# A two-layer hybrid decoder step: first loads by quarters, the table stage moved and shortened, the last gate by token parts

## Chip, cores, metric

One core of a Trainium2 chip. The metric is the device time of one execution in microseconds (us). Smaller is better. The median of the kernel before is 1286.86 us over 3 runs (1286.62 to 1287.45).

## What is computed

One inference step of a decoder with two layers, for 256 prompt tokens and 8 times 8 sample tokens (320 in all), width 1024. The reference, cut to the parts that the change touches:

```python
def layer(x, p, lw, h0, cache_k, cache_v):
    x = x + 0.5 * swiglu(rms_norm(x, lw['ffn1_norm']), lw['ffn1_w_gate'], lw['ffn1_w_up'], lw['ffn1_w_down'])
    mix, new_k, new_v, h_last = token_mixer(rms_norm(x, lw['mix_norm']), lw, h0, cache_k, cache_v)
    x = x + mix
    x = x + 0.5 * swiglu(rms_norm(x, lw['ffn2_norm']), lw['ffn2_w_gate'], lw['ffn2_w_up'], lw['ffn2_w_down'])
    gate = jax.nn.sigmoid((rms_norm(x, lw['ple_norm']) @ lw['ple_w_gate']).astype(F32))
    x = x + ((p @ lw['ple_w_proj']).astype(F32) * gate).astype(x.dtype)
    return x, new_k, new_v, h_last
...
    a_bar = jnp.exp(lam * dt)
    b_bar = ((a_bar - 1.0) / lam)[..., None] * b
...
    _, h = lax.associative_scan(_ssm_combine, (a, bu), axis=0)
...
    y_prompt = rms_norm(xp, final_norm)
```

`token_mixer` projects to u, q, k and v, runs an S5 state space model (32 groups of 16 channels with 64 complex states) on u and sliding-window attention on q, k, v, takes the RMS norm of each result and projects both back. A feed-forward part has 2816 hidden columns, 22 blocks of 128.

## The kernel before

Activations lie transposed, 128 rows of the width on the partitions and the 320 tokens along the free axis, so x is eight blocks `x[0]` to `x[7]` in one tile `xa`. Weights are streamed: SP loads a block of 128 x 1024 fp32 into one of four tiles `wr` (`wfetch`, L159), ScalarE rounds it to the high half `wh` (L163), VectorE subtracts to get the low half `wl` (L164), and two blocks are held ahead (`wtake`). The normed input of a product is split in the same way (`Norm.cut`: high half on ScalarE at L225, low half on VectorE at L226). `mm3` then makes each 128 x 128 x 320 product as three matmuls: high by high (L182), high by low (L183), low by high (L184).

A norm is never applied to the input itself. `Norm.stat` squares each block (ScalarE, L210) and adds it to `acc` (VectorE, L216); `Norm.finish` sums over partitions with matmuls by a column of ones (L244), forms the mean square on VectorE (L247) and the power -0.5 on POOL (L249). The spread of that factor over the partitions by transposes (L267) is held back by `LATER` = 22 further matmuls (24, since they come in threes), and multiplies the products when they leave PSUM.

A layer is a first feed-forward part, the mixer, a second feed-forward part and the gate (`ple`). In `ffn` the gate and up products of 12 blocks are followed by 8 down products, then 10 blocks and again 8. After each block's activation and each down product `step` asks the generator `prep` for its next piece: `prep` builds the tables of the state space model for a layer on VectorE, POOL, ScalarE and with a few transposes on TensorE, the first layer's in its own first feed-forward part (38 steps), the second layer's in the first layer's second feed-forward part. Its last pieces are the tables of cosines and sines `ect` and `est` (32 groups by 32 positions): five doublings (L579 to L584) and two renormalisations of 16 columns each (L590 to L595). `tt_d`, a table in memory, is filled with zeros (2 x 2 MB from a zeroed `wr`) before its non-zero parts are written by eight gathers.

Instructions are written in the order of this description and a scheduler places them on the engines; in the mixer a written sequence (`MIXSEQ`) sets the order of the pieces. At the start x comes in three loads and the first two weight blocks in two halves each (`HEAD`), all on SP, and the squares of the first norm are made partly on POOL (L212, L216). At the end, the eight products of the last gate are followed by the sigmoid chain of block 7 (L999 to L1002), the square, the final norm and the products with the final factor (L1058), stored in four pieces (L1059).

## Time and profile before

| | |
|---|---|
| median of 3 runs | 1286.86 us |
| profiled execution | 1286.57 us |
| its span, first to last instruction | 1284.8 us |
| granted TensorE clock, mean | 0.995 of 2.4 GHz |
| TensorE matmul / weight load busy | 98% / 96% |
| VectorE / ScalarE / POOL busy | 71% / 47% / 6% |
| memory traffic | 210.62 MB, 164 GB/s |

The profile is that of one execution. PE is TensorE, PEld its weight loads, DVE VectorE, ACT ScalarE, SP the engine that issues most loads. A row of the timeline gives the start, the duration and, in brackets, how long the engine sat idle before and what released it. Matmuls are pipelined: one of 320 columns has a duration of 0.31 us while the next starts after less than half of that, so the distance of two starts tells the pace and not the duration.

### The profile page before, as it was taken

To read this page: it belongs to the slowest core of one execution; us is meant where nothing else is said; L and a number is where in the kernel's file an instruction comes from. 1 tells how busy PE (TensorE), PEld (TensorE's weight loads), DVE (VectorE), ACT (ScalarE), POOL (GpSimd) and SP (SyncE) were. 2 spreads that over 40 slices of the span, in tenths; PEclk is the share of its full clock that TensorE was granted. 3 is DMA by queue.
4 is the path that set the end of the run, shared out by engine and by line. 5 is a ranking of instruction groups with operands and counts; after the bars stand their busy time and mean duration, and the time that the engine had idled before them with its cause. 6 is when DMAs were issued, how large, how long until landed. Compare 5 with 4: busy or idle time off the path is not lost.

```text
span 1284.8 us, 22994 instructions
## 1 busy us (share of the span) xinstructions
PE 1257.4 (98%) x9153; PEld 1231.1 (96%) x9153; DVE 911.0 (71%) x1609; ACT 598.9 (47%) x984; POOL 81.5 (6%) x96
## 2 busy tenths in 40 slices
PE   7999999899999999999999999999999999999996
PEld 7999999898899999999999999999888999999996
DVE  6588776978786878788785555557877755555575
ACT  5443433455764443344653333345476543333454
POOL 4300002001004000010000000000000000000000
PEclk9999999999999999999999999999999999999998
DMA  7836666354254468654444454345432444454351
GB/s 251 314 125 204 240 208 212 120 197 144 76 192 147 150 194 256 219 189 141 166 174 151 129 154 174 136 115 188 164 106 99 147 151 135 142 180 141 113 174 41
DMA packets 74620, 210.62 MB, mean 164 GB/s; under 512 B 8545, under 2 KB 18497, under 8 KB 74481
## 3 DMA queue, kind: packets, MB, share of 16 engines
q1 hardware_dynamic: 72560, 203.22, 47.8%
q0 software_dynamic: 1664, 5.28, 1.3%
q8 instruction: 72, 1.18, 0.4%
q10 hardware_dynamic: 288, 0.66, 0.1%
q14 instruction: 36, 0.29, 0.1%
HBM read 191.78 MB, written 19.69 MB: 165 GB/s over the span
## 4 chain that ended last, share of the span: by engine, by line
PE 89%; DVE 6%; issue 3%; ACT 1%; POOL 1%; DMA 0%; SPq 0%; POOLq 0%; DVEq 0%; ACTq 0%
PE pt L182 17%; PE pt L184 17%; PE pt L183 17%; PE pc L182 11%; PE pc L184 11%; PE pc L183 11%; DVE wl L164 2%; PE pa L872 1%; PE pa L500 1%; POOL r L249 1%; DVE s L704 0%; DVE s L703 0%; DMA xa<-xT 0%; PE pa L883 0%; PE pa L244 0%
## 5 line engine op out<-in xcount | busy, mean ns | idle before, releaser
L163 ACT ACTIVATE wh<-wr 128x1024 fp32r<-128x1024 f32 (+3 forms) x365 | 350.9, 963 | 556.3 <-issue 302.0
L184 PE MATMUL pt<-big,wl 128*128 128x320 f32 x1584 | 492.6, 311 | 4.3 <-DVE wl L164 4.3
L182 PE MATMUL pt<-big,wh 128*128 128x320 f32 x1584 | 493.4, 312 | 0.0
L183 PE MATMUL pt<-big,wh 128*128 128x320 f32 x1584 | 492.2, 311 | 0.0
L164 DVE TENSOR_TENSOR wl<-wr,wh 128x1024 fp32r<-128x1024 f32 (+3 forms) x365 | 403.1, 1107 | 100.5 <-ACT wh L163 98.5
L182 PE MATMUL pc<-big,wh 128*128 128x320 f32 x992 | 310.7, 314 | 6.7 <-ACT wh L163 6.0
L183 PE MATMUL pc<-big,wh 128*128 128x320 f32 x992 | 308.8, 312 | 0.0
L184 PE MATMUL pc<-big,wl 128*128 128x320 f32 x992 | 308.2, 311 | 0.0
L184 PEld LDWEIGHTS pt<-big,wl 128*128 128x128 f32 x1584 | 298.8, 189 | 6.0 <-DVE wl L164 5.5
L183 PEld LDWEIGHTS pt<-big,wh 128*128 128x128 f32 x1584 | 299.1, 189 | 0.5
L182 PEld LDWEIGHTS pt<-big,wh 128*128 128x128 f32 x1584 | 298.8, 189 | 0.7 <-issue 0.4
L182 PEld LDWEIGHTS pc<-big,wh 128*128 128x128 f32 x992 | 187.2, 189 | 9.6 <-ACT wh L163 6.2
L183 PEld LDWEIGHTS pc<-big,wh 128*128 128x128 f32 x992 | 187.1, 189 | 1.2 <-DVE big L226 1.2
L184 PEld LDWEIGHTS pc<-big,wl 128*128 128x128 f32 x992 | 187.2, 189 | 0.6 <-issue 0.3
L291 DVE TENSOR_TENSOR fa<-pt,ft 128x320 f32<-128x320 f32 x88 | 43.0, 489 | 91.0 <-PE pt L184 90.5
L288 DVE TENSOR_TENSOR ft<-pc,r 128x320 f32<-128x320 f32 x88 | 42.6, 488 | 53.6 <-PE pc L184 53.5
L334 DVE SCALAR_TENSOR_TENSOR fd<-pt,r 128x320 f32<-128x320 f32 x64 | 31.3, 490 | 31.6 <-PE pt L184 31.6
L249 POOL TENSOR_TENSOR r<-ms,mhalf 107x3 f32<-107x3 f32 x13 | 17.1, 1319 | 565.0 <-DVE ms L247 565.0
L225 ACT ACTIVATE big<-xa,prm 128x320 fp32r<-128x320 f32 x64 | 35.3, 559 | 31.4 <-DVE xa L335 17.4
L295 ACT ACTIVATE big<-fa 128x320 fp32r<-128x320 f32 x88 | 40.2, 459 | 14.6 <-DVE fa L291 14.5
L289 ACT ACTIVATE ft<-ft 128x320 f32<-128x320 f32 x88 | 40.0, 458 | 13.1 <-DVE ft L288 13.0
L226 DVE SCALAR_TENSOR_TENSOR big<-xa,prm,big 128x320 fp32r<-128x320 f32 x64 | 37.9, 599 | 8.4 <-ACT big L225 8.4
(246 smaller groups left out, 904.6 us busy)
## 6 DMA issues: line engine op xcount, KB each, us to landing
wr<-f1u SPq DMA_DIRECT2D x44, 512.0 KB, 3.2
wr<-f2g SPq DMA_DIRECT2D x44, 512.0 KB, 3.3
wr<-f2u SPq DMA_DIRECT2D x44, 512.0 KB, 3.3
wr<-f1g SPq DMA_DIRECT2D x43, 512.0 KB, 3.3
wr<-f1d SPq DMA_DIRECT2D x32, 384.0 KB, 3.1
wr<-f2d SPq DMA_DIRECT2D x32, 384.0 KB, 3.1
wr<-f1d SPq DMA_DIRECT2D x32, 320.0 KB, 2.9
wr<-win SPq DMA_DIRECT2D x20, 512.0 KB, 3.8
```

Of the source, the lines that this page charges most:

```text
L163: S.activation(h[:, c], raw[:, c], AF.Copy)
L164: i = V.tensor_tensor(lo[:, c], raw[:, c], h[:, c].bitcast(F32), op=OP.subtract)
L182: PE.matmul(ps, h[:, c], xh, start=start and k == 0, stop=False)
L183: PE.matmul(ps, h[:, c], xl, start=False, stop=False)
L184: PE.matmul(ps, lo[:, c], xh, start=False, stop=stop and k == n - 1)
L225: S.activation(h, src, AF.Copy, scale=g)
L226: V.scalar_tensor_tensor(lo, src, g, h.bitcast(F32), op0=OP.mult, op1=OP.subtract)
L288: V.tensor_tensor(t, pg, r, op=OP.mult)
L289: S.activation(t, t, AF.Silu)
L291: V.tensor_tensor(a, pu, t, op=OP.mult)
L295: S.activation(h, a, AF.Copy)
L334: V.scalar_tensor_tensor(t, pd, 0.5, r, op0=OP.mult, op1=OP.mult)
```

## The change

1. **Start.** x and the first two weight blocks are loaded in quarters, prm first; three quarters of x go over the queue of ScalarE. 14 matmuls of zeros (`NWARM`) run on TensorE while the loads are under way. The first pair of products is made quarter by quarter, its two results in turn. The squares of the first norm come after that pair and on ScalarE and VectorE, not on POOL.
2. **Tables.** In `prep` the stage of cosines and sines follows the powers directly. It normalises the one column of 32 elements from which the others are made, not 32 columns at the end. The products for K come before those for Wb. `kt_d` has rows of 240 with a zero part of 112, so each gather reads whole pieces of 128 and `tt_d` needs no zeros. The generator is done after 32 calls for the first layer instead of 36.
3. **Attention squares** are made per block, as soon as a block is there (`attn_stat`), not all at `attn_norm`.
4. `LATER` is 18; two loads (`h0`, `pT`) are issued after the last weight load.
5. **End.** The last gate's blocks 6 and 7 are made in two parts of 192 and 128 tokens (`CUT`). The norm's sums of part 0 run ahead of the last 24 matmuls, the final gain is applied per block, and the output is stored in two pieces of part 0 and three of part 1.

```diff
-LATER = 22
+NWARM = 14
+LATER = 18
+CUT = ((0, 192, 96), (192, 128, 128))
...
+    nc.sync.dma_start(prm, I["prm"])
+    for q in range(4):
+        (S if q < 3 else nc.sync).dma_start(xa[:, 2 * q : 2 * q + 2], I["xT"][:, 2 * q : 2 * q + 2])
+        for raw, src in zip(first, firstw):
+            headdma.append(nc.sync.dma_start(raw[:, 256 * q : 256 * q + 256],
+                                             src[:, 256 * q : 256 * q + 256]).ins)
...
+    pz = pst("po")
+    for _ in range(NWARM):
+        PE.matmul(pz[:, :T], zr_[:, :P], zr_, start=True, stop=True)
...
-                    for k0, k1 in ((0, KCUT), (KCUT, 8)):
+                    ks = (0, 2, 4, 6, 8) if head else (0, KCUT, 8)
+                    for k0, k1 in zip(ks, ks[1:]):
...
-    kt_d = [dram.tile([512, P], F32, name=f"ktd{l}") for l in range(L)]
+    kt_d = [dram.tile([512, 240], F32, name=f"ktd{l}") for l in range(L)]
...
-                nc.sync.dma_start(tt_d[ll].rearrange("p (b c) -> p b c", b=4),
-                                  zt.unsqueeze(1).to_broadcast([P, 4, 1024]))
...
+                nc.sync.dma_start(kt_d[ll].rearrange("(p b) c -> p b c", b=4)[:, :, 0:112], zt)
...
+        V.tensor_tensor(t, uc, uc, op=OP.mult)
+        V.tensor_tensor(er, us, us, op=OP.mult)
+        V.tensor_tensor(t, t, er, op=OP.add)
+        V.tensor_scalar(t, t, -0.5, 1.5, op0=OP.mult, op1=OP.add)
+        V.tensor_tensor(ct_[:, :, 1], uc, t, op=OP.mult)
+        V.tensor_tensor(sn_[:, :, 1], us, t, op=OP.mult)
...
-            PO.dma_start(dst[:, :, i * 16 :], src[:, :, : (8 - i) * 16])
+            PO.dma_start(dst, src[:, :, (7 - i) * 16 : (7 - i) * 16 + P])
...
-        for c0 in (0, 16):
-            cc, ss = ct_[:, :, c0 : c0 + 16], sn_[:, :, c0 : c0 + 16]
-            q1, q2 = auxt("s", [P, G, 16]), auxt("p", [P, G, 16])
-            V.tensor_tensor(q1, cc, cc, op=OP.mult)
-            V.tensor_tensor(q2, ss, ss, op=OP.mult)
-            V.tensor_tensor(q1, q1, q2, op=OP.add)
-            V.tensor_scalar(q1, q1, -0.5, 1.5, op0=OP.mult, op1=OP.add)
-            V.tensor_tensor(cc, cc, q1, op=OP.mult)
-            V.tensor_tensor(ss, ss, q1, op=OP.mult)
...
         def attn_norm():
-            for m in range(4):
-                na.stat(ya[:, m, :])
...
+        if tail is not None:
+            ws = [wtake(), wtake()]
+            pgs = [pst("pc")[:, :T], pst("pt")[:, :T]]
+            for i, ts in enumerate(slice(t0, t0 + n) for t0, n, _ in CUT):
+                xt = [(h[:, ts], lo[:, ts]) for h, lo in xs]
+                for m, w, pg in zip((6, 7), ws, pgs):
+                    mm3(pg[:, ts], *w, 0, xt, True, True)
+                    if i == 1 and m == 6:
+                        tail.sums(0)
+                    gate(m, pg, ts)
+                    tail.stat(i, m, ts)
+            tail.behind = done[-1]
...
+    last.sums(1)
+    last.out(0, ((0, 3), (3, 8)))
+    last.out(1, ((0, 3), (3, 6), (6, 8)))
```

How the instructions move is shown at three places. Line numbers of the changed kernel are its own: L207 to L209 are `mm3`'s three matmuls, L173 the low half of a weight block, L371, L372, L256 and L246 what were L334, L335, L226 and L216.

TensorE at the start of the program, after the change (`zr` is a tile of zeros, `pc` and `pt` the two results of the first pair):

```order
L106 MATMUL po_102<-zr 128x320 x14
L207 MATMUL pc_194<-big_146,wh_142 128x320
L208 MATMUL pc_194<-big_147,wh_142 128x320
L207 MATMUL pt_195<-big_146,wh_144 128x320
L208 MATMUL pt_195<-big_147,wh_144 128x320
L209 MATMUL pc_194<-big_146,wl_143 128x320
```

Before, the program began on TensorE with the products of `pc` alone; now the zeros come first, and products of both results follow as their quarter is there.

VectorE at the end of the first feed-forward part of layer 0, in the second half's down steps, before (`ect`, `est` are the cosines and sines, `wl` the low half of a weight block that TensorE takes next):

```order
L584 TENSOR_TENSOR est_2527<-p_2685,p_2686 128x32x15
L164 TENSOR_TENSOR wl_2697<-wr_2694,wh_2696 128x640
L164 TENSOR_TENSOR wl_2718<-wr_2715,wh_2717 128x640
L334 SCALAR_TENSOR_TENSOR fd_2736<-pt_2693,r_306 128x320
L590 TENSOR_TENSOR s_2744<-ect_2526 128x512
L335 TENSOR_TENSOR xa<-xa,fd_2736 128x320
L591 TENSOR_TENSOR p_2745<-est_2527 128x512
L164 TENSOR_TENSOR wl_2756<-wr_2753,wh_2755 128x640
```

and the same place after the change:

```order
L371 SCALAR_TENSOR_TENSOR fd_2674<-pt_2631,r_335 128x320
L372 TENSOR_TENSOR xa<-xa,fd_2674 128x320
L173 TENSOR_TENSOR wl_2707<-wr_2704,wh_2706 128x640
L256 SCALAR_TENSOR_TENSOR big_2610<-xa,prm,big_2609 128x320
L246 TENSOR_TENSOR acc_2613<-acc_2613,sq_2679 128x320
L173 TENSOR_TENSOR wl_2737<-wr_2734,wh_2736 128x640
```

No product of the tables is left between the low halves.

TensorE at the end of the program, after the change (`po` and `pa` hold the sums and the spread factor; 24 matmuls of 128 columns for block 7 stand between the two groups of L1110):

```order
L209 MATMUL pc_14166<-big_13752,wl_14089 128x128
L1110 MATMUL pa_14257<-ones,acc_14025 96x1
L1110 MATMUL pa_14257<-ones,sq_14230 96x1
...
L209 MATMUL pt_14167<-big_13752,wl_14129 128x128
L1110 MATMUL po_14307<-ones,acc_14025 128x1
L1122 MATMUL pa_14314<-ident,r_2381_14264 128x96 x2
L1110 MATMUL po_14307<-ones,sq_14304 128x1
L1122 MATMUL po_14323<-ident,r_2388_14312 128x128
```

Before, the six sums and the three transposes all stood behind the last matmul; now four sums stand ahead of the last 24.

## Rows read from the trace of the kernel before

**Rows 1.** The page: busy time by engine; the chain's shares
```profile
PE 1257.4 (98%) x9153; PEld 1231.1 (96%) x9153; DVE 911.0 (71%) x1609; ACT 598.9 (47%) x984; POOL 81.5 (6%) x96
...
PE 89%; DVE 6%; issue 3%; ACT 1%; POOL 1%; DMA 0%; SPq 0%; POOLq 0%; DVEq 0%; ACTq 0%
```

**Rows 2.** TensorE's waits: engine, line, awaited line, total us, times, longest
```profile
PE pc L182 <- ACT wh L163: 6.0, 1, 6.0
PE pt L184 <- DVE wl L164: 4.3, 4, 1.9
PE pa L267 <- POOL r L249: 4.3, 5, 1.3
```

**Rows 3.** Timeline of TensorE in the head
```profile
17.22 0.47 PE L182 MATMUL pt<-big,wh 128*128 128x320 f32 x1
17.48 0.47 PE L183 MATMUL pt<-big,wh 128*128 128x320 f32 x1
...
19.57 0.31 PE L182 MATMUL pt<-big,wh 128*128 128x320 f32 x1
...
31.32 0.31 PE L184 MATMUL pc<-big,wl 128*128 128x320 f32 x1
```

**Rows 4.** Busy time by stretch: us, PE, PEld, DVE, ACT, POOL, clock, DMA share, GB/s
```profile
222.00:258.00 36.00, 31.88 (x201) 30.72 (x200) 35.77 (x87) 15.48 (x26) 1.21 (x4) 0.95 0.41 126
66.00:108.00 42.00, 42.00 (x288) 42.00 (x287) 37.78 (x111) 16.23 (x23) 0.00 (x0) 1.00 0.40 123
241.40:244.80 3.40, 3.40 (x14) 3.40 (x14) 3.40 (x7) 1.55 (x3) 0.00 (x0) 0.50 0.61 191
```

**Rows 5.** Timeline of TensorE, table stage
```profile
238.05 0.31 PE L183 MATMUL pt<-big,wh 128*128 128x320 f32 x1
240.24 0.41 PE L184 MATMUL pt<-big,wl 128*128 128x320 f32 x1 [1.88 <-DVE wl L164]
```

**Rows 6.** Timeline of VectorE, same stage
```profile
228.69 0.30 DVE L583 TENSOR_TENSOR ect<-s,s 128x128 f32<-128x128 f32 x1
...
230.61 0.55 DVE L226 SCALAR_TENSOR_TENSOR big<-xa,prm,big 128x320 fp32r<-128x320 f32 x1
...
239.37 1.55 DVE L164 TENSOR_TENSOR wl<-wr,wh 128x640 fp32r<-128x640 f32 x2
...
241.24 0.68 DVE L590 TENSOR_TENSOR s<-ect 128x512 f32<-128x512 f32 x1
```

**Rows 7.** Timeline of ScalarE and VectorE in the head
```profile
4.06 1.01 ACT L225 ACTIVATE big<-xa,prm 128x320 fp32r<-128x320 f32 x2 [1.82 <-DMA prm<-prm]
...
5.99 0.68 DVE L164 TENSOR_TENSOR wl<-wr,wh 128x512 fp32r<-128x512 f32 x1
...
11.51 1.74 DVE L164 TENSOR_TENSOR wl<-wr,wh 128x1024 fp32r<-128x1024 f32 x1
```

**Rows 8.** Timeline of TensorE at a norm in layer 0's mixer
```profile
348.20 0.40 PE L183 MATMUL pc<-big,wh 128*128 128x320 f32 x1
...
349.74 0.49 PE L267 MATMUL pa<-ident,r 107*128 107x107 f32 x3 [0.86 <-POOL r L249]
```

**Rows 9.** Timeline of the end: last two blocks and what follows
```profile
1264.72 0.31 PE L182 MATMUL pc<-big,wh 128*128 128x320 f32 x1
...
1271.61 0.31 PE L184 MATMUL pt<-big,wl 128*128 128x320 f32 x1
...
1274.56 0.35 PE L244 MATMUL pa<-ones,sq 128*107 128x1 f32 x2 [2.54 <-ACT sq L210]
...
1276.01 0.85 POOL L249 TENSOR_TENSOR r<-ms,mhalf 107x3 f32<-107x3 f32 x1 [24.41 <-DVE ms L247]
...
1277.75 3.01 DVE L1058 TENSOR_TENSOR big<-xa,pa 128x320 f32<-128x320 f32 x4 [1.82 <-PE pa L267]
```

**Rows 10.** Timeline of TensorE: narrow operations of layer 0
```profile
109.79 1.04 PE L500 MATMUL pa<-ident,s 128*128 128x128 f32 x8
...
325.97 0.66 PE L811 MATMUL pt<-kv,qs 128*128 128x64 f32 x4
```

More of the change, by code (lines that the diff above doesn't have):

```diff
@@ L1 @@
 import math
-from contextlib import ExitStack
+from contextlib import ExitStack, nullcontext
 import numpy as np
@@ L174, in wtake @@
         return wready.pop(0)
-    waiting = []
+    waiting, held = [], []
     def mm3(ps, h, lo, off, pairs, start, stop):
@@ L187, in mm3 @@
                 if waiting[0][0] <= 0:
-                    waiting.pop(0)[1]()
+                    with tc.issue_after(mm.ins):
+                        waiting.pop(0)[1]()
     class Norm:
@@ L236, in pairs, with finish @@
             ]
-        def finish(self, then=None):
+        def finish(self, then=None, hold=0):
             ps = pst("pa")
@@ L243, in finish @@
                 for i, a in enumerate(sums):
-                    PE.matmul(ps[:SN, c : c + 1], a[:, t0 : t0 + SN], ones, start=i == 0,
+                    mm = PE.matmul(ps[:SN, c : c + 1], a[:, t0 : t0 + SN], ones, start=i == 0,
                               stop=i == len(sums) - 1)
@@ L260, in later @@
                 then(r)
-            waiting.append([LATER, later])
+            waiting.append([hold or LATER, later])
+            if hold:
+                held[:] = [mm.ins, hold]
         def spread(self, r4):
@@ L269, in spread, with ffn @@
             return pr[:, :T]
-    def ffn(l, idx, pre, post, side=None, after=3):
+    def ffn(l, idx, pre, post, side=None, after=3, head=False):
         xs = pre.pairs()
@@ new lines, in hybrid_step_kernel @@
+    pre = Norm(8, lambda m: gcol(0, GF1, m))
+    for raw in first:
+        next(wsrc)
+        wready.append((wpool.tile([P, 1024], F32R, name=nm("wh"), tag="wh", bufs=WB),
+                       wpool.tile([P, 1024], F32R, name=nm("wl"), tag="wl", bufs=WB)))
+    lastdma.extend(headdma)
+    for q in range(4):
+        pre.cut(2 * q, x[2 * q])
+        for raw, (h, lo) in zip(first, wready):
+            wsplit(h, lo, raw, slice(256 * q, 256 * q + 256))
+        pre.cut(2 * q + 1, x[2 * q + 1])
```

317 lines of the change are left out of this document (188 added, 129 removed).

## The prediction

> **What bounds the kernel now.** I read the page's busy shares first and its chain of waits second [rows 1]: TensorE is busy for 98% of the span and the chain that ends last lies on it for 89%, VectorE for 6%. The reader is to see that VectorE, at 71%, is far from full as an average, so a microsecond is worth something only where TensorE does not run at its usual pace. The next view, TensorE's own waits [rows 2], says how few such places there are: one long wait for the first split weights, 4.3 us in four waits for the low half of a weight block (L164), and 4.3 us in five waits for a norm's power (L249), of which the last belongs to the program's end.
>
> Then the timeline of each place. At the usual pace matmuls of 320 columns start 0.147 us apart: 47 intervals between 1264.72 and 1271.61 [rows 9]. **Head:** at 17.22 and 17.48 they start 0.26 apart, at 31.32 the 114th of them starts [rows 3]. At 0.147 each, 114 would take 16.8 us, so the first 31 us hold some 14 us that are not matmuls at pace: waiting for data until 5.99 (the one 6.0 wait [rows 2]), gaps, and the slow pace until 19.35. **Table stage:** between 222 and 258 us VectorE is busy for 35.77 of 36 us and TensorE for 31.88 [rows 4]; a matmul that should start at 238.20 starts at 240.24, behind L164 [rows 5], which itself stands behind the table's products on VectorE [rows 6]. From 241.4 to 244.8 the granted clock is 0.50, its lower level of 1.2 GHz, right after that idle stretch [rows 4]. **Tail:** from the last matmul's start at 1271.61 to the end of the span at 1284.8 are 13.2 us of one short chain after another [rows 9].
>
> **The change part by part.** All sums are against the profiled execution, 1286.57 us (span 1284.8 and 1.8 outside it); the median of the three runs is 0.3 higher.
>
> *Head.* ScalarE and VectorE must make the split inputs and weights of the first pair whatever the size of the loads. Per quarter ScalarE has two L225 (1.01 for two) and two splits of 256 columns, at about 0.4 each: 1.8 us [rows 7]. VectorE has two residuals at 0.55 [rows 6] and two splits at about 0.4 each, from 0.68 for 512 columns [rows 7], which I take for ScalarE too: 1.9. Before, the loads came in another order and POOL's squares ran beside VectorE, where a split of 1024 took 1.74 [rows 7], 1.7 ns a column against 1.2 in the 1.55 for two of 640 [rows 6]. ScalarE starts at 4.06 now, when prm is there; I keep that, since prm is now first and the first part of x is as large as it was. Four quarters at 1.85 and VectorE's lag of 0.6 put the last piece at 12.1 and the 48th product at 13.0. The 14 matmuls of zeros cost 14 times 0.267, 3.7 us, from about 1.5, when VectorE has made the zeros, to 5.25, in time in which TensorE had nothing to do. With them TensorE works almost without a pause from 1.5 on. Before, the fast pace began only at 19.57, when it had run back to back since 15.9; I expect it by about 8. Then 56 products at 0.147 (8.2) reach the 104th, three sums 0.5, nine products 1.3, a wait of 0.5 for the power, since nine products cover less than the 1.5 that this chain takes in the mixer (from 348.20, the first matmul behind the sums, to 349.74 [rows 8]) and VectorE has a split ahead of it, and 0.45 of transposes: the 114th starts at 24.2 instead of 31.32, **-7.1**. Bounds: if the slow pace holds through all 48 products, 12.8 us from 5.3 on, they end at 18.1 and the gain is 2.0; if the splits come faster and it is never slow, 7.9. The squares of the first norm, moved to ScalarE and VectorE, lie behind the splits of the next weights and have 56 products of cover: nothing.
>
> *Tables.* Twelve products of 512 columns go (L590 to L595, 0.68 each [rows 6]), replaced by six of 32 columns, and the rest of that stage moves into the first twelve activation steps. In the last six down steps VectorE then has only its two splits (1.55 together), and four operations near 0.4 to 0.5: 3.2 us in a step whose 30 matmuls take 4.4. So no wait stays there. The four waits cost 4.3, some 0.12 more each from start to start (2.04 for the longest, where the row says 1.88), 4.8; the 14 matmuls at the lower clock took 3.4 us, 2.06 at the usual pace, 1.3. Together **-6.1**. What it costs if the cover is gone: from 66 to 108 us VectorE was already busy for 37.78 of 42 us [rows 4]. Priced with such rows, the table work of the generator's calls 6 to 12 comes to some 23 us; seven steps of 48 matmuls are 49.3 us, of which VectorE's own two splits and three operations leave about half, 24.7. The 4 MB of zeros that went to memory from SP become 0.46 MB; the loads that follow on SP are not late, since two blocks are held ahead. The eight gathers on POOL stay eight. The same generator in layer 0's second FFN caused no wait before and is shorter now: nothing.
>
> *Norms in the mixer.* The attention squares leave VectorE's queue ahead of the sums, so the sums come earlier: 14 matmuls ahead of the third, but then four before the transposes where three stood. The chain from sums to transposes is as long, and its wait (0.86 at 349.74 [rows 8]) is shortened by one matmul in each layer: **-0.3** for both. The order around it is changed too; I bound that by 1 us a layer either way. The delay of 18 instead of 24 matmuls elsewhere still covers the chain: nothing.
>
> *Tail.* 48 matmuls of 320 columns become 48 of 192 and 48 of 128. The trace has no narrow product of this kind. The nearest row is the transposes of 128 by 128 that load 128 columns of weights each [rows 10]: eight in 1.04 us, the last taking 0.27, so 0.110 apart. 96 times 0.110 is 10.6 against 48 times 0.147, 7.05: +3.5. I take that value for both widths, since every matmul still loads 128 columns. Bounds: 0.147, as for the wide ones, +7.1; and in proportion to the columns (0.088 and 0.059), nothing. Four more sums calls in mid-stream, whose two records take 0.35 [rows 9] and overlap their neighbours for more than half of it, 0.15 each: +0.6. After the last matmul, 2.95 us to the sums before [rows 9] were 0.35 to the first operation and five steps of 0.52; five of 0.33 for 128 columns (0.30 for one on VectorE [rows 6]) make 2.0; one sums call, ms and power (0.85) lead to 3.65; one transpose to 4.1; 1024 columns of final products instead of 2560 (3.01), 1.3; then 4.0 from the last product to the end as now, less 0.2 for a smaller store: 9.2 instead of 13.2, -4.0. The sum is **+0.1**.
>
> The Trainium skill, "TensorE: Matmul & The Clock Gate", section "Back-to-back issue gap", gives about 81 ns per matmul for a sustained stream of load and matmul at 128 columns; by it the 96 would take 7.8, an estimate, 2.8 less than in the sum, and the time would be 1270.4. The trace's 0.110 for 128 columns is against it, so the sum goes by the row.
>
> Sum: -7.1, -6.1, -0.3, +0.1 are -13.4: **1273.2 us**.
>
> **The rivals.**
> - *The clock does not rise early,* or the smaller loads land late, at the same price. The 14 matmuls are worth nothing and the pace stays at 0.267 through the head pair: gain 2.0 instead of 7.1, 1278.3. For it: the fast pace came late before. Against: then TensorE had pauses, now hardly any. 0.13.
> - *The table stall moves.* VectorE falls behind in the activation steps instead; for it, that only 1.7 us of 24.7 are left. Against: there a step has 48 matmuls and the splits run two blocks ahead. In full it takes back 6.1, 1279.3; half is as likely. 0.14.
> - *Narrow matmuls keep the wide pace.* If 0.147 is set by something that does not depend on columns, the tail costs 3.6 more: 1276.8. Against: the transposes' 0.110. 0.11.
> - *Narrow matmuls go by their columns.* At 0.088 and 0.059 the tail costs 3.5 less: 1269.7. Against: the same row, and that PEld is busy for 96% of the span [rows 1], so that loads lie close behind the matmuls. The 81 ns of the Trainium skill's section named above lie between the two paces. 0.10.
> - *Other side: a narrow matmul runs in two passes,* as the fp32 products of L811 do: two calls leave four records [rows 10]. They take 0.66 us, 0.128 apart, so 0.26 a call; with 1.5 of that for 192 columns, 96 cost 31, 20 more than forecast: 1293, slower. It decides above a mean of 0.25 us, since 13.4 and 10.6 over 96 is that. Against: the 320-column products of the same type leave one record each. 0.02.
>
> **How the numbers follow.** Forecast 0.50, which leaves the rivals' 0.50. The forecast's own range is 1270.5 to 1275.5: 1 us for the head's pieces, 1 for the mixer's order, 0.5 for the tail. With the late clock, the moved stall and either pace of the narrow matmuls the range is 1269 to 1279.5. No change is what differs by less than 0.2%, 2.6 us, about what a measurement of this kernel can tell. Two rivals at once (late clock and moved stall, 1284.4) still are just faster; three, or the two passes, are not. Faster 0.94, same 0.03, slower 0.03.
>
> **What would show it.** Right, if the changed profile has the 114th product near 24, the fast pace by 8 us, no wait for the split's low half in 222 to 258 and the clock at 1.00 there; narrow matmuls 0.11 apart, and some 9 us from the last one's start to the end. Wrong, if waits for L173 appear between 60 and 110 us, or if matmuls in the first pair start 0.267 apart to its end, or if the last two blocks' narrow ones stand 0.147 or more apart.

## The result and the profile after

The changed kernel takes 1278.09 us (median of four runs, 1277.98 to 1278.62), the kernel before 1287.15 beside it; the ratio is 0.9932, 95% interval 0.9919 to 0.9944. It is faster, by 9.1 us where 13.4 were forecast; 1278.09 lies inside the whole range (1269 to 1279.5), 4.9 above the predicted time and outside the forecast's own range of 1270.5 to 1275.5. The profiled execution took 1277.98, its span is 1276.2.

The page, to be read beside [rows 1]: TensorE still bounds the kernel, and the share of VectorE in the chain has halved.

```profile
PE 1259.1 (99%) x9215; PEld 1232.2 (97%) x9215; DVE 902.5 (71%) x1620; ACT 603.6 (47%) x1001; POOL 69.0 (5%) x86
...
PE 94%; DVE 3%; DMA 1%; issue 1%; ACT 1%; POOL 0%; SPq 0%; POOLq 0%; DVEq 0%; ACTq 0%
```

Where the time came from is read by one instruction that both kernels have, the mean square of a norm on VectorE: its start after, less its start before. Four of them, in the first rows of the kernel before and then of the changed one: the norm behind layer 0's first feed-forward part, the one behind its mixer, and the same two of layer 1.

```profile
268.16 0.16 DVE L247 TENSOR_SCALAR ms<-pa 107x3 f32<-107x3 f32 x1 [2.33 <-PE pa L244]
391.82 0.16 DVE L247 TENSOR_SCALAR ms<-pa 107x3 f32<-107x3 f32 x1 [4.51 <-PE pa L244]
893.77 0.16 DVE L247 TENSOR_SCALAR ms<-pa 107x3 f32<-107x3 f32 x1 [4.50 <-PE pa L244]
1017.33 0.16 DVE L247 TENSOR_SCALAR ms<-pa 107x3 f32<-107x3 f32 x1 [4.50 <-PE pa L244]
```

```profile
256.80 0.16 DVE L277 TENSOR_SCALAR ms<-pa 107x3 f32<-107x3 f32 x1 [4.43 <-PE pa L274]
381.46 0.16 DVE L277 TENSOR_SCALAR ms<-pa 107x3 f32<-107x3 f32 x1 [4.50 <-PE pa L274]
883.45 0.16 DVE L277 TENSOR_SCALAR ms<-pa 107x3 f32<-107x3 f32 x1 [4.50 <-PE pa L274]
1007.98 0.16 DVE L277 TENSOR_SCALAR ms<-pa 107x3 f32<-107x3 f32 x1 [4.51 <-PE pa L274]
```

The lead is 11.36 us at the first, 10.36 at the second, 10.32 at the third, 9.35 at the fourth, and 8.6 in the span. From 40 to 100 us TensorE's products lead by 4.57. So the head gave 4.6, the table stage 6.8; each mixer took back 1.0; the tail took back 0.7.

| step | forecast | measured |
|---|---|---|
| head | -7.1 | -4.6 |
| tables | -6.1 | -6.8 |
| mixers, both | -0.3 | +2.0 |
| tail | +0.1 | +0.7 |
| sum | -13.4 | -8.6 |

**Head**, TensorE, beside [rows 3]:

```profile
1.77 4.10 PE L106 MATMUL po<-zr 128*128 128x320 f32 x14 [1.77 <-DVE zr L103]
5.94 0.55 PE L207 MATMUL pc<-big,wh 128*128 128x320 f32 x1
7.15 0.41 PE L207 MATMUL pt<-big,wh 128*128 128x320 f32 x1 [0.51 <-ACT wh L172]
...
14.77 0.42 PE L207 MATMUL pc<-big,wh 128*128 128x320 f32 x1 [0.45 <-ACT wh L172]
16.04 0.41 PE L207 MATMUL pt<-big,wh 128*128 128x320 f32 x1 [0.72 <-ACT wh L172]
...
26.68 0.39 PE L209 MATMUL po<-big,wl 128*128 128x320 f32 x1
```

From 7.55 us on matmuls start 0.147 apart. The 48th product starts at 14.01 (forecast 13.0), the 114th, the last of these rows, at 26.68 (forecast 24.2). In between TensorE waits twice for the second pair of weight blocks. ScalarE's rows say what it waits for itself, the loads:

```profile
5.47 0.42 ACT L172 ACTIVATE wh<-wr 128x256 fp32r<-128x256 f32 x1 [0.97 <-DMA wr<-f1g]
6.68 0.42 ACT L172 ACTIVATE wh<-wr 128x256 fp32r<-128x256 f32 x1 [0.79 <-DMA wr<-f1u]
...
13.66 1.06 ACT L172 ACTIVATE wh<-wr 128x1024 fp32r<-128x1024 f32 x1 [1.54 <-DMA wr<-f1g]
14.93 1.06 ACT L172 ACTIVATE wh<-wr 128x1024 fp32r<-128x1024 f32 x1 [0.22 <-DMA wr<-f1u]
```

SP, the engine that issues these loads, does so at 7.57 and 7.94; the kernel before issued its second pair at 4.02 and 4.49:

```profile
7.57 0.33 SPq L182 DMA_DIRECT2D wr<-f1g  x1
7.94 0.43 SPq L182 DMA_DIRECT2D wr<-f1u  x1
```

```profile
4.02 0.43 SPq L159 DMA_DIRECT2D wr<-f1g  x1
4.49 0.88 SPq L159 DMA_DIRECT2D wr<-f1u  x1
```

In the compiled program the loads of SP and ScalarE take turns over eight semaphores, and a load waits until the one eight places ahead of it has landed: the load of 7.57 follows the second quarter of f1g, which landed at 7.55. The kernel before has seven first loads (its second weight block comes whole, not in halves as the words ahead say), the changed one 13, so the second pair waits.

**Table stage**, the windows beside [rows 4]: nothing is idle, the clock stays at 1.00, and VectorE has 10 us to spare where it had none. The stretch that now has the stage, 60 to 130, is not idle either:

```profile
222.00:258.00 36.00, 36.00 (x249) 36.00 (x248) 26.06 (x44) 19.76 (x31) 0.95 (x1) 1.00 0.62 208
...
60.00:130.00 70.00, 70.00 (x512) 68.83 (x511) 66.17 (x146) 26.04 (x35) 1.20 (x2) 1.00 0.53 163
```

**TensorE's waits**, beside [rows 2]: no low half of a weight (it would be L173) is left. A norm's power (L279) is still there twice. The wait of L828 for VectorE's L817, in the mixer, is new to this list, and L700, which was L669 before with 0.3, has grown to 0.9.

```profile
PE pa L299 <- POOL r L279: 1.7, 2, 0.9
PE pt L828 <- DVE s L817: 1.2, 2, 0.6
...
PE pa L700 <- DVE big L683: 0.9, 4, 0.3
```

**Mixer**, layer 0's attention norm in the changed kernel, beside [rows 8]: the transposes of L299 stand four matmuls behind the last sums (336.31) and wait 0.87, 1.17 us from start to start, no less than before.

```profile
336.96 0.30 PE L209 MATMUL pc<-big,wl 128*128 128x320 f32 x1
338.13 0.49 PE L299 MATMUL pa<-ident,r 107*128 107x107 f32 x3 [0.87 <-POOL r L279]
```

**Tail**, beside [rows 9]. Two neighbouring narrow matmuls of each width, the last one of part 1 and what follows on TensorE, and VectorE's last products:

```profile
1255.47 0.28 PE L208 MATMUL pc<-big,wh 128*128 128x192 f32 x1
1255.58 0.27 PE L209 MATMUL pc<-big,wl 128*128 128x192 f32 x1
...
1260.80 0.27 PE L208 MATMUL pc<-big,wh 128*128 128x128 f32 x1
1260.91 0.28 PE L209 MATMUL pc<-big,wl 128*128 128x128 f32 x1
...
1266.62 0.27 PE L209 MATMUL pt<-big,wl 128*128 128x128 f32 x1
...
1268.67 0.38 PE L1110 MATMUL po<-ones,sq 128*128 128x1 f32 x2 [1.39 <-ACT sq L1096]
...
1270.00 0.47 PE L1122 MATMUL po<-ident,r 128*128 128x128 f32 x1 [0.95 <-POOL r L1115]
...
1270.52 1.35 DVE L1128 TENSOR_TENSOR big<-xa,po 128x384 f32<-128x384 f32 x3
```

Both widths start 0.111 apart, 0.110 forecast. The last starts 9.6 before the end of the span (forecast 9.2).

### The profile page after: what moved, and what is told of

Its sections match the earlier page's. It is cut to its first block, busy times and chain, and to the rows that moved or that the text cites. A ratio compares the mean times of both kernels' runs of the same rounds, so it can differ in the third digit from the quotient of the medians.

```text
span 1276.2 us, 23133 instructions
## 1 busy us (share of the span) xinstructions
PE 1259.1 (99%) x9215; PEld 1232.2 (97%) x9215; DVE 902.5 (71%) x1620; ACT 603.6 (47%) x1001; POOL 69.0 (5%) x86
## 4 chain that ended last, share of the span: by engine, by line
PE 94%; DVE 3%; DMA 1%; issue 1%; ACT 1%; POOL 0%; SPq 0%; POOLq 0%; DVEq 0%; ACTq 0%
PE pt L207 18%; PE pt L208 18%; PE pt L209 18%; PE pc L207 11%; PE pc L208 11%; PE pc L209 11%; PE pa L924 1%; PE pa L624 1%; DMA wr<-f1u 1%; PE po L837 0%; PE pa L274 0%; DVE wl L173 0%; PE pt L828 0%; DMA wr<-f1g 0%; DVE s L734 0%
## 5 line engine op out<-in xcount | busy, mean ns | idle before, releaser
L207 PE MATMUL pt<-big,wh 128*128 128x320 f32 x1592 | 493.3, 310 | 1.2 <-ACT wh L172 1.2
L209 PE MATMUL pt<-big,wl 128*128 128x320 f32 x1592 | 491.9, 309 | 0.0
L173 DVE TENSOR_TENSOR wl<-wr,wh 128x1024 fp32r<-128x1024 f32 (+3 forms) x370 | 402.8, 1091 | 118.0 <-ACT wh L172 116.1
L207 PE MATMUL pc<-big,wh 128*128 128x320 f32 (+1 forms) x992 | 309.0, 312 | 0.5 <-ACT wh L172 0.5
L208 PE MATMUL pc<-big,wh 128*128 128x320 f32 (+1 forms) x992 | 306.7, 309 | 0.0
L209 PE MATMUL pc<-big,wl 128*128 128x320 f32 (+1 forms) x992 | 306.5, 309 | 0.0
L207 PEld LDWEIGHTS pt<-big,wh 128*128 128x128 f32 x1592 | 298.9, 188 | 3.6 <-ACT wh L172 1.8
L209 PEld LDWEIGHTS pt<-big,wl 128*128 128x128 f32 x1592 | 299.0, 188 | 0.1
L207 PEld LDWEIGHTS pc<-big,wh 128*128 128x128 f32 x992 | 186.3, 188 | 2.4 <-ACT wh L172 1.2
L209 PEld LDWEIGHTS pc<-big,wl 128*128 128x128 f32 x992 | 186.3, 188 | 0.4 <-issue 0.3
L371 DVE SCALAR_TENSOR_TENSOR fd<-pt,r 128x320 f32<-128x320 f32 x64 | 31.4, 491 | 37.0 <-PE pt L209 37.0
L279 POOL TENSOR_TENSOR r<-ms,mhalf 107x3 f32<-107x3 f32 x12 | 14.8, 1232 | 598.5 <-DVE ms L277 598.5
L328 DVE TENSOR_TENSOR big<-fa,big 128x320 fp32r<-128x320 f32 x88 | 42.7, 486 | 1.1 <-ACT big L327 1.1
```

The costliest lines, as they stand in the source:

```text
L173: lastwl.append(V.tensor_tensor(lo[:, c], raw[:, c], h[:, c].bitcast(F32), op=OP.subtract).ins)
L207: PE.matmul(ps, h[:, c], xh, start=start and k == 0, stop=False)
L208: PE.matmul(ps, h[:, c], xl, start=False, stop=False)
L209: mm = PE.matmul(ps, lo[:, c], xh, start=False, stop=stop and k == n - 1)
L328: V.tensor_tensor(lo, a, h.bitcast(F32), op=OP.subtract)
L371: V.scalar_tensor_tensor(t, pd, 0.5, r, op0=OP.mult, op1=OP.mult)
```

## The experiments

"Offset" below is the start of the same instruction in an experiment less that in the changed kernel. Seven executions with an unchanged head have the 114th product between 25.71 and 27.28 us: the head alone varies by over 1 us from one execution to the next, so mixers and tail are read as differences of offsets behind it. By and large that product comes late where the second weight pair lands late: from 25.71, with f1u's block landed at 13.62, to 27.28, with 15.14. The tail varies too: in eight executions in which it is the same, what it adds to the offset differs by 0.3. The kernel before took 1286.87 to 1286.96 beside the runs below that have its number.

### The mixers: LATER and the squares by block

Theory: `LATER` at 18 is what costs a microsecond a layer. Rival: the squares by block, which move the pieces of the mixer against each other. First the squares, all at the norm again:

```diff
-                attn_stat(self.m)
...
-                    attn_stat(None)
...
         def attn_norm():
+            for m in range(4):
+                na.stat(ya[:, m, :])
```

> The changed kernel with the attention squares made all at once at the norm again; nothing else. Theory (the squares per block move the mixer's middle into an order with more waits): the stretch of each mixer between the eleven or twelve products and the last attention mix takes 16.9 us again instead of 17.9, the second norm wait of about 0.9 us comes back, and the net is 0.7 us a layer, 1.4 in all: 1276.7. Rival (the middle's loss comes from the delayed loads or from LATER, not from the squares): the middle stays at 17.9 and the norm wait comes back, 1278.7.

Measured: 1277.60 (four runs), ratio to before 0.9926 [0.9911, 0.9941]. Its head was 0.96 earlier; the offsets fell by 0.48 in layer 0's mixer and 0.49 in layer 1's. So, with `LATER` at 18, the squares by block cost half a microsecond a layer, where the theory said 0.7: TensorE's 0.89 behind L817 at 310.88 becomes 0.53, although the norm's power is now waited for four times (3.4 us) instead of twice (1.7). The other half is something else. Then `LATER` alone:

```diff
-LATER = 18
+LATER = 22
```

> The changed kernel with the spread of a norm's factor after 22 matmuls again instead of 18. Theory (what the mixers lost beside the squares comes from the earlier spread, which puts a transposition of the first projection before VectorE has made its input): the wait of 0.59 there is 0.36 again, 0.25 us a layer, and the wait for the attention norm's power, 1.18 us behind 4 matmuls, shrinks to about 0.3 behind 10, 0.85 us a layer unless the products behind it then wait: 0.5 to 2.2 us earlier in all. Rival (neither): the same times at both places.

Measured: 1275.47 in one run, span 1273.7, with a head 0.61 later. The offsets fall by 1.55 and 1.56 in the two mixers, 0.90 of it in layer 0 between the attention norm and the norm behind it. The waits of L700 fall from 0.9 to 0.3. The wait of the changed kernel at 338.13 is gone; the transposes stand ten matmuls behind the last sums instead of four, with no wait:

```profile
338.13 0.31 PE L209 MATMUL pc<-big,wl 128*128 128x320 f32 x1
338.43 0.40 PE L299 MATMUL pa<-ident,r 107*128 107x107 f32 x2
```

The two runs and the two kernels make a table of layer 0's mixer against the kernel before (layer 1 is within 0.04 of it; the changed kernel's +1.00 less 0.48, and less 1.55):

| | squares at the norm | squares by block |
|---|---|---|
| `LATER` 22 | 0 (before) | -0.55 |
| `LATER` 18 | +0.52 | +1.00 (changed) |

Neither theory alone says this: the squares by block gain with the long delay and lose with the short one, and the short delay costs 0.52 without them and 1.55 with them. The last column and the last row are runs of the changed kernel; the first cell is the kernel before, which differs from it in more (two loads issued later, the order around the held-back transposes), so the 0.52 and the gain of 0.55 are shown only as far as that costs nothing. `LATER` is what has to be undone.

### The table stage: amount or place

Theory: the place of the stage decides. Rival: its amount, that is, the shortened normalisation. In the kernel before, the short normalisation alone:

```diff
-        V.tensor_copy(ct_[:, :, 1], uc)
-        V.tensor_copy(sn_[:, :, 1], us)
+        V.tensor_tensor(t, uc, uc, op=OP.mult)
+        V.tensor_tensor(er, us, us, op=OP.mult)
+        V.tensor_tensor(t, t, er, op=OP.add)
+        V.tensor_scalar(t, t, -0.5, 1.5, op0=OP.mult, op1=OP.add)
+        V.tensor_tensor(ct_[:, :, 1], uc, t, op=OP.mult)
+        V.tensor_tensor(sn_[:, :, 1], us, t, op=OP.mult)
...
-        for c0 in (0, 16):
...
```

> The kernel before with one part of the change alone: the normalisation of one column instead of 32 columns of the tables, in its old place at the end. Theory A (the amount of work on VectorE at the end decides): twelve products of 0.6 go of some 17 us there, the rest fits into the free 1.2 us a step with what is held ahead, and the waits of 4.3 us and the slow clock vanish or nearly: 1281 to 1282. Theory B (the place decides, since the doublings of 0.65 alone hold up the low halves): the two first waits, of 1.5 and 1.9 us, stay, and the slow clock with them: 1284 to 1285.

Measured: 1287.33 over ten runs (1284.92 to 1291.99), ratio 1.0005 [0.9993, 1.0017]: no change. At the end of the first feed-forward part it leads before by 7.82, of which 1.01 in the head, so the whole 6.8 of the table stage. That is not the smaller amount at work, since the stage has left the down steps: VectorE makes L569 at 223.00 and goes on with L570 only at 262.70 (555.97 and 593.56 in layer 1). L570 writes `er` anew, which POOL's copy to `dec` (L560) reads; that copy had ended at 221.18, so it was not waited for, and why the scheduler orders L570 so late is not shown. So no run has the short normalisation in the old place. Then the lead is given back twice. The scheduler put the stage into the first 10 us of the mixer, where VectorE runs from 262.70 through to 272.44 with little else, and TensorE waits for L646 behind it (3.4 us lost up to 348 us):

```profile
262.70 0.18 DVE L570 TENSOR_TENSOR er<-us 128x32 f32<-128x32 f32 x1
...
271.87 0.64 DVE L588 TENSOR_TENSOR est<-p,p 128x480 f32<-128x480 f32 x1
272.44 0.76 DVE L646 TENSOR_TENSOR big<-pc,r 128x320 f32<-128x320 f32 x1
```

```profile
273.34 1.79 PE L663 MATMUL pa<-ident,big 128*40 128x128 f32 x8 [2.09 <-DVE big L646]
...
605.74 0.39 PE L182 MATMUL pt<-big,wh 128*128 128x320 f32 x1 [1.33 <-DVE fd L334]
607.63 0.41 PE L184 MATMUL pt<-big,wl 128*128 128x320 f32 x1 [1.36 <-DVE wl L164]
```

The second layer's stage, without a wait before, fell into layer 0's last down steps (the last two rows) and cost 5.0 more. Then the reverse, the long normalisation in the new place:

```diff
-        V.tensor_tensor(t, uc, uc, op=OP.mult)
...
+        V.tensor_copy(ct_[:, :, 1], uc)
+        V.tensor_copy(sn_[:, :, 1], us)
...
+        for c0 in (0, 16):
+            cc, ss = ct_[:, :, c0 : c0 + 16], sn_[:, :, c0 : c0 + 16]
...
+            yield
```

> The changed kernel with the old normalisation of 32 columns (twelve products, six calls more to VectorE, two more calls of the generator) in the new, early place of the stage. Theory (the place decides): the six down steps at the end of the first feed-forward part have nothing of it, the activation steps that take it have spare time on VectorE; the first feed-forward part loses under 1 us against the changed kernel, no wait for L173 in 60 to 130 us. Rival (the amount decides): VectorE, with 1.7 us to spare by my count, gets 5.7 us of products more (twelve of 0.68 less six small ones) and TensorE stalls by 3 to 6 us in activation steps 6 to 14. Time by the theory 1278 to 1279, by the rival 1281 to 1284; the head varies by up to 1 us from run to run.

Measured: 1278.25 in one run. The offset grows by 0.27 in the first feed-forward part and not at all in layer 0's second (the 0.17 that it grows in the gate behind it is also in two runs below that leave the tables alone, 0.20 in each). VectorE is fuller, TensorE as busy as before:

```profile
60.00:130.00 70.00, 69.94 (x499) 68.89 (x498) 68.47 (x148) 25.55 (x35) 1.20 (x2) 1.00 0.49 151
```

In the new place the rival falls: 68.47 of 70 us on VectorE cost next to nothing there. The place, with the rest of the generator's new order, gave 6.5 of the 6.8, and the shorter normalisation behind it 0.3. Alone it gave nothing, since its edit moved the stage to two places that are worse; whether it would have been enough in the old place no run shows.

### The head: zeros and loads

Theory when the first of these was written: the zeros gave little, the loads set the head. Rival: without them the slow pace lasts. Taken away: the 14 matmuls of zeros and the tile they read.

```diff
-    pz = pst("po")
-    for _ in range(NWARM):
-        PE.matmul(pz[:, :T], zr_[:, :P], zr_, start=True, stop=True)
```

> The changed kernel without the 14 matmuls of zeros at its start (their result is used by nobody). Theory (they bring the fast pace forward, but the first pair is then bound by the splits' supply): the first products start at 5.9 as now, 0.267 apart for some microseconds, and the 114th comes 0.5 to 1.6 us later than 26.7: 1278.6 to 1279.7. Rival A (without them the pace is slow through the whole first pair): the 48th product at 18.7 instead of 14.0, 1282. Rival B (the loads alone set the head): no change, 1278.1.

Measured: 1281.90 (1279.63 to 1283.15), ratio 0.9958 [0.9941, 0.9974]; offset +3.76 in the head. The theory falls, and the time is the rival's (1282):

```profile
12.89 0.47 PE L201 MATMUL pt<-big,wh 128*128 128x320 f32 x1
13.16 0.44 PE L202 MATMUL pt<-big,wl 128*128 128x320 f32 x1
13.43 0.32 PE L200 MATMUL pc<-big,wh 128*128 128x320 f32 x1
13.59 0.31 PE L201 MATMUL pc<-big,wh 128*128 128x320 f32 x1
```

Matmuls start 0.267 apart until 13.4 and 0.147 after; with the zeros the fast pace is there at 7.55. So the slow pace did not last through the whole pair: the 48th product comes at 16.81 instead of 14.01, where the rival said 18.7.

The 114th comes at 30.52 instead of 26.68, and the late pace itself is the smaller part of that, since the changed kernel waits for the second pair's weights meanwhile: 56 products at 0.147 from 16.81 on and the changed kernel's last 2.76 us would reach 27.8, 1.1 later. The rest are two waits at the first norm (0.45 for its sums, 0.74 for its power; the scheduler put the sums behind 95 products instead of 104) and a second slow stretch: from 27.1 to 30.5 matmuls start 0.267 apart again, at a granted clock of 0.50, which costs 1.5 us. Without the zeros the change would keep 0.8 of its head.

Nor do the zeros always bring the pace by 7.55: in the run below that splits block 7 alone, with the zeros in place, matmuls start 0.267 apart until 11.2, and the 114th still comes at 26.78, since the second pair's weights land no earlier there (13.72 and 15.01).

What is left is the late second pair. Three ways to have it earlier. Seven larger first loads, so that nothing has to wait for the eighth place:

```diff
-    for q in range(4):
-        (S if q < 3 else nc.sync).dma_start(xa[:, 2 * q : 2 * q + 2], I["xT"][:, 2 * q : 2 * q + 2])
+    for x0, x1, w0, w1 in ((0, 2, 0, 256), (2, 5, 256, 1024), (5, 8, 0, 0)):
+        S.dma_start(xa[:, x0:x1], I["xT"][:, x0:x1])
...
+            if w1:
+                headdma.append(nc.sync.dma_start(raw[:, w0:w1], src[:, w0:w1]).ins)
```

> The changed kernel with fewer first loads: x in parts of 2, 3 and 3 blocks, the two weight blocks in 256 and 768 columns, seven loads beside prm instead of twelve. The splits and products stay in quarters. Theory (a new load must wait until the one eight places earlier has landed, so that twelve small loads hold back the loads of the next two weight blocks): these are issued before 4.8 us instead of 7.57 and 7.94, land before 12, the gaps of 0.76 and 1.02 us at 14.0 to 16.0 go, and the 114th product comes 1.3 to 1.8 us earlier: 1276.5. Rival (memory traffic sets when the second pair of weights lands): they land at 13.7 and 14.9 as now, 1278.1.

Measured: 1280.10 (1279.56 to 1280.81), ratio 0.9947 [0.9932, 0.9962]; offset +1.95. The second pair is issued at 3.97 and 4.35 and the waits at 14 to 16 are gone, as expected. But the first quarter of the second weight block, which let TensorE go on at 7.15, lands later, and TensorE, which starts nothing between 6.6 and 8.5, then runs at the lower clock:

```profile
8.05 0.42 ACT L172 ACTIVATE wh<-wr 128x256 fp32r<-128x256 f32 x1 [1.74 <-DMA wr<-f1u]
```

```profile
8.50:12.00 3.50, 3.48 (x13) 3.48 (x14) 2.66 (x6) 2.56 (x7) 0.00 (x0) 0.53 1.02 416
```

The quarters as they were, and only the second pair's loads moved to POOL's queue:

```diff
-        lastdma.append(nc.sync.dma_start(raw[:, :n], src).ins)
+        eng = PO if len(lastdma) < len(headdma) + 2 else nc.sync
+        lastdma.append(eng.dma_start(raw[:, :n], src).ins)
```

> The changed kernel with the loads of the second pair of weight blocks issued by POOL, whose loads are counted apart, and everything else as it is. Theory (eight loads at a time): they are issued near 2 us, land before 12 unless they slow the first quarters, and the gaps at 14.0 to 16.0 go: 1276.5 to 1277.5. Since they then share the memory with the first quarters from 2 us on, the first pair may end later by up to 1 us. Rival (memory traffic): no change, 1278.1, or slower.

Measured: 1282.45 (1281.98 to 1284.17), ratio 0.9968 [0.9955, 0.9981]; offset +4.13. The second pair is issued at 1.82 and 2.55; that first quarter is split at 8.10 instead of 6.68, and a later one makes TensorE wait until 12.49; from 9.0 to 13.7 matmuls start 0.267 apart, which is part of the loss. All loads in SP's queue, the other way round:

```diff
-        (S if q < 3 else nc.sync).dma_start(xa[:, 2 * q : 2 * q + 2], I["xT"][:, 2 * q : 2 * q + 2])
+        nc.sync.dma_start(xa[:, 2 * q : 2 * q + 2], I["xT"][:, 2 * q : 2 * q + 2])
```

> The changed kernel with the three quarters of x that ScalarE's queue loads moved to SP's queue, in the same order of quarters. Theory after the two runs on loads (loads that are under way at once share the memory, and x's second and third quarter delay the first weights): in one queue they land about in the order of issue, as in the kernel before; the first f1u quarter lands near 5.5 instead of 6.68, the 48th product starts near 13.0 instead of 14.0, and the second pair's weights land no later than 13.7; the kernel ends 0.8 to 1.5 us earlier. Rival (the eight-at-a-time rule or SP's issue of about 0.45 us each holds back the last quarters): the last quarter lands after 11, the 48th product after 14, no gain or a loss of up to 2 us.

Measured: 1278.10 (1277.93 to 1278.17), ratio 0.9930 [0.9914, 0.9947]; offset +0.06. The first quarter of f1u lands earlier (5.37 instead of 6.66), the last one later (12.49 instead of 10.80). The waits are elsewhere, their sum is the same. The three agree on one cause, which the windows of the changed kernel show too: from 2 to 16 us its DMA engines are busy for 0.97 of the time (the column before the last).

```profile
2.00:16.00 14.00, 12.29 (x64) 10.94 (x64) 7.97 (x17) 10.03 (x21) 0.00 (x0) 1.00 0.97 309
```

Loads that are under way together share the DMA engines. A later load that starts sooner makes the first ones land later, and the rule of eight at a time, which I took for the fault, protects the first pair. Busy engines are not yet all that memory gives, though: in the changed kernel 0.97 is 309 GB/s, and the run with seven larger loads moves 416 in the window shown, at 1.02. Its second pair, issued earlier, lands at 12.00 and 13.23 instead of 13.64 and 14.91. Whether the small quarters make that difference was not tried by itself. The Trainium skill, "DMA: Bandwidth & Descriptors", section "Issuing engines are not separate DMA queues", says that loads started by different engines "will ultimately run on the same 16 DMA engines and interleave with each other"; the run with POOL's queue agrees, its first quarter 1.4 us later.

### The tail

Theory: the 48 narrow matmuls of block 6 cost more than they hide. Block 6 made whole, block 7 alone in two parts:

```diff
-        for m in range(8 if tail is None else 6):
+        for m in range(8 if tail is None else 7):
...
-                for m, w, pg in zip((6, 7), ws, pgs):
...
+                mm3(pg[:, ts], *w, 0, xt, True, True)
+                gate(7, pg, ts)
+                tail.stat(i, 7, ts)
+            tail.sums(0)
```

> The changed kernel with block 6 of the last gate in one part of 320 tokens again, and block 7 alone in parts of 192 and 128. Theory (each narrow matmul takes 0.111 us whatever its width, and only the last group's width sets the chain after it): 24 matmuls of 0.147 take the place of 48 of 0.111, the four sums of part 0 go behind the last product beside its chain, and the last product's start to the end stays near 9.6: 2.0 us earlier than the changed kernel. Rival (the first part's norm is now late too and its outputs hold VectorE): the end is 1 us longer, gain 1.0.

Measured: 1277.73 (1277.36 to 1278.13), ratio 0.9928 [0.9913, 0.9942]. The tail is 0.7 shorter, nearer to the rival's 1.0 than to the theory's 2.0. The scheduler put a first sums call between block 7's two parts, where it waits for a sum of squares that is not there yet, 0.87 from start to start, and the power is then waited for twice behind the last matmul, 1.15 and 1.27:

```profile
1262.45 0.30 PE L1107 MATMUL pa<-ones,acc 128*96 128x1 f32 x2 [0.59 <-DVE acc L246]
...
1269.42 0.47 PE L1119 MATMUL po<-ident,r 128*128 128x128 f32 x1 [1.27 <-POOL r L1112]
```

The tail of the kernel before, in the changed kernel (the last gate whole, one norm behind it, four stores):

```diff
-            last = Last()
-            ple(l, nple, last.add, last)
-    last.sums(1)
-    last.out(0, ((0, 3), (3, 8)))
-    last.out(1, ((0, 3), (3, 6), (6, 8)))
+            pre = Norm(8, None, split=False)
+            ple(l, nple, lambda m: pre.add(m, x[m]))
+    r = pre.finish()
...
```

> The changed kernel with the tail of the kernel before: the last gate whole, one norm behind it, the final factor applied in products after ScalarE's gain, four stores. My theory: the split tail cost 0.74 us, so this run is 0.7 us shorter from the last gate's start to the end (1277.3 with the head as it was). Rival (the prediction's own sum, +0.1): no difference that can be seen, under 0.2 us.

Measured: 1277.38 in one run, span 1275.6: its tail is 0.26 shorter than the changed one, between theory and rival, and within what the changed tail varies by. The same tail took 0.48 less in the kernel before (13.19 from the last matmul's start to the end, here 13.67), and its rows show where: the five sums calls stand 0.36 apart, in the kernel before 0.19, at a granted clock of 0.50 here (the window's third number from the end) and of 0.87 in 1274.5 to 1276.0 there, behind the same idle 2.54 us. So the final products start 0.85 later than in the kernel before, and from their end to that of the span 0.36 less passes.

```profile
1264.80:1267.00 2.20, 1.96 (x10) 1.87 (x10) 0.04 (x1) 0.60 (x2) 0.00 (x0) 0.50 0.00 0
```

So the split tail cost 0.3 to 0.7, by the kernel that it is compared with; the 0.3 is no more than one tail varies by, and only the 0.7 is clear of that.

### The repairs together

`LATER` at 22, block 7 alone split, and the sums of part 0 behind the last product:

```diff
+            with tc.issue_after(lastmm[0]):
+                tail.sums(0)
```

> The changed kernel with LATER at 22 and, in the tail, block 7 alone split, with the sums of part 0 issued behind the last product. Theory: the mixers give 3.1 us, as LATER 22 alone gave; the tail 1.6 us (0.74 for block 6 whole and the 0.87 us that TensorE waited between the two parts of block 7 in the run that split block 7 alone). Against the changed kernel -4.7, so 1273.4 (span 1271.5). Rival: with the sums behind the last product, the wait for the power comes in full behind them, and the tail gives 0 to 0.7 only: 1274.3 to 1275.

Measured: 1274.45 (1274.44 to 1275.50, four runs), ratio to before 0.9902 [0.9886, 0.9919], the fastest of all. In the profiled execution the mixers gave 1.51 each, as expected; the tail gave nothing and cost 0.26 (0.28 in the run below, which has the same one). The rival holds, and its price was even too kind: the power is waited for in full, and the clock fell to 0.54 during the last matmuls and the sums, so the sums stood 0.32 apart instead of 0.17. Nor did the edit take the wait between the two parts away: the scheduler put a sums call of part 1 there (1259.50), 0.78 from start to start where it was 0.87.

```profile
1262.10:1264.00 1.90, 1.90 (x14) 1.90 (x12) 0.29 (x1) 0.31 (x1) 0.00 (x0) 0.54 0.00 0
```

```profile
1265.20 0.58 PE L1121 MATMUL pa<-ident,r 96*128 96x96 f32 x2 [1.09 <-POOL r L1114]
```

The same with seven loads in SP's queue, in the order in which they are needed:

```diff
+    for x0, x1, w0, w1 in ((0, 2, 0, 256), (2, 5, 256, 1024), (5, 8, 0, 0)):
+        nc.sync.dma_start(xa[:, x0:x1], I["xT"][:, x0:x1])
```

> The run above with the seven first loads in one queue, in the order in which they are needed (x part 0, first quarters of both weight blocks, x part 1, the rest of the weights, x part 2), so that the second weight pair does not wait for an eighth load. Theory: the first quarters land as early as in the changed kernel, since nothing else is ahead of them in that queue, and the gaps at 14 to 16 us shrink: the head gains 0.5 to 1.5 us against the run above, about 1272.4. Rival: loads under way at once share the memory whatever their queue, the first quarters land 1 to 1.5 us later as with seven loads in two queues, and the head loses 1 to 2 us: 1274.5 to 1275.5.

Measured: 1275.14 (1274.57 to 1275.99), ratio 0.9908 [0.9893, 0.9923]: no difference from the run above that can be told. The first quarters of the weights do come in time now and the waits at 14 to 16 are gone, but the second part of x lands late, and TensorE is idle for 2.18 us before 10.08. The 114th product comes at 26.53. In no order of these loads that was tried did it come earlier than in the seven heads left unchanged (25.7 to 27.3).

## Why the prediction was right, and where its sum was wrong

The direction and the whole range held. That the range held is partly luck: the forecast's own, 1270.5 to 1275.5, was missed by 2.6, and 1278.09 is inside the wider one only by the room made for rivals that did not come true. The time fell beside the price of the first rival (1278.3, a late clock), but not by its mechanism: the fast pace came at 7.55, as the forecast said ("by about 8"). Four errors make up the 4.8 us.

- **Head, forecast -7.1, measured -4.6 (in this execution).** The step that failed is the one that counts only engines: "Four quarters at 1.85 and VectorE's lag of 0.6 put the last piece at 12.1". The splits are faster than that, 1.52 a quarter on ScalarE and 1.6 on VectorE. But ScalarE waits 0.97 and 0.79 for the first weight quarters, TensorE can start on the second result only at 7.15, and from 7.55 on the products need their 0.147 each: 14.01 instead of 13.0. Then "56 products at 0.147 (8.2)" took 9.9, since the second pair's weights were late; the sum had no term for a load behind the first pair. From the 104th product to the 114th it was right (2.76 us, forecast 2.75). The terms as written add up to 23.95 and not to the 24.2 that the sum goes on with, a slip of 0.25 in the forecast's favour. The zeros were worth 3.8 us in the executions compared; the first rival's 2.0 against 7.1 had put them at 5.1.
- **Tables, forecast -6.1, measured -6.8.** Right in mechanism and nearly in size: no wait for a low half from 222 to 258, the clock at 1.00, no wait in 60 to 130. The reason given for it was half wrong. That twelve products go gave 0.3 once the stage stood elsewhere; where it stands gave the rest, and VectorE had more room there than the 1.7 us that were counted, for the old normalisation fitted too.
- **Mixers, forecast -0.3, measured +2.0.** The failed step is "The delay of 18 instead of 24 matmuls elsewhere still covers the chain: nothing." It does not, in the mixer, and with the squares by block it is worth 1.55 a layer, though alone, by the table above, only 0.52: two edits of the change, priced one by one, work on each other. Nor was the wait at the attention norm "shortened by one matmul": four stand in front of it instead of three, and it is 0.87 where it was 0.86. The bound of 1 us a layer either way held at its bad end (1.00 and 0.97); the value taken inside it was wrong in sign.
- **Tail, forecast +0.1, measured +0.7.** The new kind of instruction was priced right: 0.111 apart, from the transposes' 0.110 [rows 10]. Both rivals on its pace fall, as do the two passes. From the first narrow matmul to the last it took 11.24 against 6.89 (+4.35, forecast +4.1), and the end 9.59 against 13.19 (-3.60, forecast -4.0): from the end of the last final products to that of the span 4.3 passed, where 3.8 were taken. The 81 ns of the Trainium skill's "TensorE: Matmul & The Clock Gate", section "Back-to-back issue gap", are not seen here: two widths, 192 and 128 columns, have the same 0.111, and the wide ones have 0.147. So the pace at the two narrow widths is not set by their columns; that the weight load sets it, as the forecast argued, fits but no run separates it from other fixed costs.

What stays open: why the second pair's loads, and the head with them, land at different times in executions of one head, and whether a tail with block 6 whole and the sums in their old place inside block 7's second part would keep the 0.7 without the 0.87 us wait; that was not tried.

## What to carry to other kernels

A helper engine's work is priced by where it stands, not by how much of it there is: a stage with less work that fell into steps without room gained nothing here, and the full stage in steps with room lost 0.3. A cover given in matmuls (`LATER`) has to be checked against the chain at every place where it is used; six matmuls less cost 3.1 us of 1278 here, about two thirds of it, by the table above, only because another edit came with it. Where first loads already keep the DMA engines busy, the orders and cuts tried here moved the waits, and what helped was to give TensorE something to do until they land.

## What was not expected of the hardware

- 14 matmuls on zeros, 4.1 us of work that computes nothing, took 3.8 us off the kernel: without them matmuls stood 0.267 apart until 13.4 us, with them 0.147 from 7.55. Not all of it is that early pace: 1.5 us is a second stretch at 0.267 (27.1 to 30.5), behind waits of 0.45 and 0.74.
- The records of the head without zeros give a clock of 1.00 from 5 to 15 us although matmuls stand 0.267 apart until 13.4, and 0.50 from 27.1 to 30.5 at the same pace: in the first microseconds the pace tells more than the clock column.
- Loads under way together delay each other: issuing the second pair over 5 us earlier (1.82 instead of 7.57) made the first quarter of f1u land 1.4 us later and the kernel 4 us slower, in part at the slower pace.
- A matmul of 128 by 128 weights takes 0.111 from start to start with 128 columns and with 192, and 0.147 with 320.
